# Attention on one core: weights times V as Strassen's seven products in 2x2 blocks, laid between score tiles, with the order of all engines written by hand

## The chip, the cores and the metric

The kernel runs on one core of one Trainium2 chip. The metric is the device time of one launch in microseconds (us), the median over runs; lower is better. The core has a matrix engine (TensorE, PE in the profile; its weight loads are PEld), VectorE (DVE), ScalarE (ACT), GpSimd (POOL) and SyncE (SP); POOL and SP here only issue transfers, apart from a few memsets.

## The reference

```python
scores = np.matmul(q, k.transpose(0, 2, 1)) / np.sqrt(d_k)
attn_weights = special.softmax(scores, axis=-1).astype(np.float32)
return np.matmul(attn_weights, v)
```

q, k and v are float32 of 8 batches x 2048 rows x 512 columns, drawn from a normal distribution. The result is float32 of the same shape.

## The kernel before, in words

Each batch has 16 blocks of 128 rows of K and V (`NKB`), 4 query tiles of 512 rows (`NQT`, `QTW`) and 4 chunks of 128 in the depth of 512 (`ND`). Everything on TensorE is float16, sums are float32.

`prep_dma(b)` asks for a batch's K and Q in two halves each and for V in one piece, through POOL's queue; the transfers turn float32 into float16. V has one more column, set to 1, so that the product with it also gives the row sums of the weights.

`prep_tr(b)` turns K and Q so that depth lies on the partitions: for batch 0 on TensorE (transposes against an identity, lines 83, and a VectorE copy out of PSUM, line 88), for later batches by transposing transfers on SP's queue (line 93), eight per batch, asked for after query tile 0 of the batch before.

`main_batch(b)` goes through the query tiles. For each, 16 score tiles `stp` of 128 x 512 are made by four matmuls each (line 107), and ScalarE writes exp(score / sqrt(512)) into `ptall` as float16 (line 114); there is no subtraction of a maximum. Then for each of four row blocks of 128 queries (`qs`), 32 matmuls add up weights times V over the 16 K blocks in two PSUM banks: line 126 for 257 columns with the column of ones, line 130 for the other 256. VectorE takes the reciprocal of the row sum (line 135), scales 512 columns (line 138) and SP's queue stores the block (line 140).

The pools have 3 score tiles, 2 pairs of output banks, 1 bank for transposes, 2 buffers of `ptall` and 4 of the scaled output. The Tile framework sets the semaphores and orders each engine's instructions by priority; within TensorE all scores of a query tile come ahead of its products with V.

Of the kernel before, what the change touches and what calls it, by code (L numbers as in the profile page):

```python
# [1 line left out]

# [1 line left out]

# [5 lines left out]


@with_exitstack
def kernel(
    ctx: ExitStack,
    tc: tile.TileContext,
    q: bass.AP,
    k: bass.AP,
    v: bass.AP,
    out: bass.AP,  # L20
):
    nc = tc.nc
    P = 128
    B, T, D = q.shape
    F16 = mybir.dt.float16
    F32 = mybir.dt.float32

    NKB = T // P
    ND = D // P
    QTW = 512  # L30
    NQT = T // QTW
    NQS = QTW // P
    NB_ = 256
    NA_ = D + 1 - NB_
    inv_sqrt_d = float(1.0 / np.sqrt(D))
    GP = min(8, NKB)
    NG = NKB // GP

    const = ctx.enter_context(tc.tile_pool(name="const", bufs=1))
    prep_pool = ctx.enter_context(tc.tile_pool(name="prep", bufs=1))  # L40
    persist = ctx.enter_context(tc.tile_pool(name="persist", bufs=2))
    pt_pool = ctx.enter_context(tc.tile_pool(name="ptp", bufs=2))
    oout_pool = ctx.enter_context(tc.tile_pool(name="oout", bufs=4))
    st_psum = ctx.enter_context(tc.tile_pool(name="st_ps", bufs=3, space=bass.MemoryType.PSUM))
    o_psum = ctx.enter_context(tc.tile_pool(name="o_ps", bufs=2, space=bass.MemoryType.PSUM))
    tr_psum = ctx.enter_context(tc.tile_pool(name="tr_ps", bufs=1, space=bass.MemoryType.PSUM))

    ident = const.tile([P, P], F16)

    prepared = {}  # L50
    TG = 4

    def prep_dma(b):
        qh = prep_pool.tile([P, NKB, D], F16, tag="qh")
        kh = prep_pool.tile([P, NKB, D], F16, tag="kh")
        vh = persist.tile([P, NKB, D + 1], F16, tag="vh")
        nc.vector.memset(vh[:, :, D:D + 1], 1.0)  # L57
        qsrc = q[b].rearrange("(n p) d -> p n d", p=P)
        ksrc = k[b].rearrange("(n p) d -> p n d", p=P)
        vsrc = v[b].rearrange("(n p) d -> p n d", p=P)  # L60
        for g in range(NG):
            ts = slice(g * GP, (g + 1) * GP)
            nc.gpsimd.dma_start(out=kh[:, ts, :], in_=ksrc[:, ts, :])  # L63
            nc.gpsimd.dma_start(out=qh[:, ts, :], in_=qsrc[:, ts, :])  # L64
        nc.gpsimd.dma_start(out=vh[:, :, 0:D], in_=vsrc)  # L65
        prepared[b] = [qh, kh, vh, None, None]

    def prep_tr(b):
        st = prepared[b]
        qh, kh = st[0], st[1]  # L70
        qtT = persist.tile([P, NKB, ND, P], F16, tag="qtT")
        ktT = persist.tile([P, NKB, ND, P], F16, tag="ktT")
        st[3] = qtT
        st[4] = ktT
        if b == 0:
            for g in range(NG):
                for src, dst in ((kh, ktT), (qh, qtT)):
                    for j in range(0, GP, 2):
                        tb = g * GP + j
                        trp = tr_psum.tile([P, 2, ND, P], F16, tag="trp")  # L80
                        for jj in range(2):
                            for dc in range(ND):
                                nc.tensor.transpose(  # L83
                                    trp[:, jj, dc, :],
                                    src[:, tb + jj, dc * P:(dc + 1) * P],
                                    ident,
                                )
                        nc.vector.tensor_copy(out=dst[:, tb:tb + 2], in_=trp[:])  # L88
            return
        for g in range(NKB // TG):  # L90
            ns = slice(g * TG, (g + 1) * TG)
            for src, dst in ((kh, ktT), (qh, qtT)):
                nc.sync.dma_start_transpose(  # L93
                    out=dst[:, ns].rearrange("p n c r -> p (n c) r"),
                    in_=src[:, ns, :].rearrange("p n d -> p (n d)"),
                )

    def main_batch(b):
        if b + 1 < B:
            prep_dma(b + 1)  # L100
        _, _, vh, qtT, ktT = prepared[b]
        for qt in range(NQT):
            ptall = pt_pool.tile([P, NKB, QTW], F16, tag="ptall")
            for kb in range(NKB):
                stp = st_psum.tile([P, QTW], F32, tag="stp")
                for dc in range(ND):
                    nc.tensor.matmul(  # L107
                        stp[:],
                        ktT[:, kb, dc, :],
                        qtT[:, qt * NQS:(qt + 1) * NQS, dc, :],  # L110
                        start=(dc == 0),
                        stop=(dc == ND - 1),
                    )
                nc.scalar.activation(  # L114
                    out=ptall[:, kb, :],
                    in_=stp[:],
                    func=mybir.ActivationFunctionType.Exp,
                    scale=inv_sqrt_d,
                )
            for qs in range(NQS):  # L120
                op = o_psum.tile([P, 2 * 512], F32, tag="op")
                opA = op[:, 512:512 + NA_]
                opB = op[:, 0:NB_]
                for kb in range(NKB):
                    lhs = ptall[:, kb, qs * P:(qs + 1) * P]
                    nc.tensor.matmul(  # L126
                        opA, lhs, vh[:, kb, NB_:NB_ + NA_],
                        start=(kb == 0), stop=(kb == NKB - 1),
                    )
                    nc.tensor.matmul(  # L130
                        opB, lhs, vh[:, kb, 0:NB_],
                        start=(kb == 0), stop=(kb == NKB - 1),
                    )
                rinv = oout_pool.tile([P, 1], F32, tag="rinv")
                nc.vector.reciprocal(out=rinv[:], in_=op[:, 512 + NA_ - 1:512 + NA_])  # L135
                osb = oout_pool.tile([P, D], F32, tag="osb")
                src = op.rearrange("p (a c) -> p a c", c=512)[:, :, 0:NB_]
                nc.vector.tensor_scalar_mul(out=osb[:], in0=src, scalar1=rinv[:])  # L138
                gq = qt * NQS + qs
                nc.sync.dma_start(  # L140
                    out=out[b, gq * P:(gq + 1) * P, :], in_=osb[:]
                )
            if qt == 0 and b + 1 < B:
                prep_tr(b + 1)

    prep_dma(0)
    ident_dram = nc.inline_tensor(
        np.eye(P, dtype=np.float16), name="attn_identity"
    )
    nc.sync.dma_start(out=ident[:], in_=ident_dram.ap())  # L150
    prep_tr(0)
    for b in range(B):
        main_batch(b)


# [1 line left out]
_INS = ['q', 'k', 'v']  # L157
_OUTS = [((8, 2048, 512), 'float32')]


# [23 lines left out]
```

## Time and profile before

| what | before |
|---|---|
| time, median of 3 runs | 936.78 us (936.47 to 937.01) |
| time of the profiled execution | 936.28 us |
| its span, first to last instruction | 934.5 us |
| PE busy | 909.8 us, 97% |
| DVE busy | 128.8 us, 14% |
| ACT busy | 306.9 us, 33% |
| transfers | 114.19 MB, mean 122 GB/s |
| mean granted TensorE clock | 0.996 |

The profile page lists busy time per engine, the chain of work that ended last, and groups of equal instructions by line with their count, busy time and mean duration. [...] SPq and POOLq are the queues of SP and POOL. In a table by stretches (windows) the columns are the stretch, its length, each engine's busy time with its number of instructions in the order PE, PEld, DVE, ACT, POOL, then the granted clock, the mean number for the transfers and GB/s.

### The profile page before, as it was taken

What the parts mean: (1) busy time and instruction counts of PE and PEld (TensorE: products, weight loads), DVE (VectorE), ACT (ScalarE), POOL (GpSimd) and SP (SyncE); (2) the same over time, 40 slices, a digit from 0 to 9 for tenths busy, and PEclk for the clock granted to TensorE, in tenths of its full rate; (3) what the DMA queues carried; (4) which work ended last, traced back from release to release, by engine and by line L of the source; (5) the groups of instructions that cost most, each with busy time, mean ns of one, the idle gap of its engine ahead of it and who ended that gap; (6) DMA issues with size and microseconds to landing.
All of it is one profiled execution on the core that took longest, in us unless ns stands there. A gap on an engine that the chain in (4) does not pass through costs nothing.

```text
span 934.5 us, 13963 instructions
## 1 busy us (share of the span) xinstructions
PE 909.8 (97%) x6272; PEld 610.8 (65%) x6272; DVE 128.8 (14%) x280; ACT 306.9 (33%) x513; POOL 37.5 (4%) x44
## 2 busy tenths in 40 slices
PE   3997999999999999999999999999999999999998
PEld 2666666677666677666677666677666677766676
DVE  2211111111011111101111101111110111111111
ACT  0430444222444222344322344322344322344321
POOL 2101000100001000000001000010000000000000
PEclk9998999999999999999999999999999999999999
DMA  9999939980599417991199901998039411000111
GB/s 167 207 193 194 230 84 180 209 160 34 97 184 220 99 47 128 198 205 57 46 169 188 207 35 49 192 213 167 26 82 188 112 46 46 35 23 34 46 46 46
DMA packets 184908, 114.19 MB, mean 122 GB/s; under 512 B 119312, under 2 KB 168464, under 8 KB 184848
## 3 DMA queue, kind: packets, MB, share of 16 engines
q0 software_dynamic: 49792, 50.33, 34.0%
q1 hardware_dynamic: 135056, 62.96, 29.7%
q8 instruction: 49, 0.80, 0.3%
q14 instruction: 11, 0.09, 0.0%
HBM read 100.70 MB, written 33.55 MB: 144 GB/s over the span
## 4 chain that ended last, share of the span: by engine, by line
PE 90%; DMA 5%; SPq 3%; issue 1%; POOL 0%; DVE 0%; POOLq 0%; DVEq 0%
PE stp L107 44%; PE op L126 23%; PE op L130 23%; DMA kh<-in_k_dram 4%; SPq L93 3%; DMA out_dram<-osb 0%; DVE osb L138 0%; POOL kh L63 0%; POOL qh L64 0%; SPq L140 0%; DVE rinv L135 0%; POOLq L63 0%; DVEq L138 0%; POOLq L168 0%; POOLq L64 0%
## 5 line engine op out<-in xcount | busy, mean ns | idle before, releaser
L114 ACT ACTIVATE ptall<-stp 128x512 f16<-128x512 f32 x512 | 305.7, 597 | 609.0 <-PE stp L107 609.0
L126 PE MATMUL op<-vh,ptall 128*128 128x257 f16 x2048 | 455.3, 274 | 5.1 <-DVE osb L138 5.1
L130 PE MATMUL op<-vh,ptall 128*128 128x256 f16 x2048 | 455.2, 273 | 0.0
L107 PE MATMUL stp<-qtT,ktT 128*128 128x512 f16 x2048 | 450.5, 380 | 0.0
L107 PEld LDWEIGHTS <-ktT 128*128 128x128 f16 x2048 | 200.4, 98 | 233.4 <-issue 1.1
L126 PEld LDWEIGHTS <-ptall 128*128 128x128 f16 x2048 | 199.6, 97 | 36.9 <-DVE osb L138 5.7
L130 PEld LDWEIGHTS <-ptall 128*128 128x128 f16 x2048 | 200.2, 98 | 29.4
L135 DVE RECIPROCAL rinv<-op 128x1 f32<-128x1 f32 x128 | 21.5, 168 | 749.4 <-PE op L130 749.4
L138 DVE TENSOR_SCALAR osb<-op,rinv 128x512 f32<-128x512 f32 x128 | 96.1, 751 | 26.5 <-DMA out_dram<-osb 22.4
L65 POOL DMA_DIRECT2D vh<-in_v_dram x8 | 9.2, 1156 | 481.6 <-DVE osb L138 425.9
L63 POOL DMA_DIRECT2D kh<-in_k_dram x16 | 14.2, 887 | 175.2 <-DMA ktT<-kh 100.9
L83 PE MATMUL trp<-ident,kh 128*128 128x128 f16 x64 | 6.6, 266 | 12.8 <-DMA kh<-in_k_dram 10.5
L83 PEld LDWEIGHTS <-kh 128*128 128x128 f16 x64 | 5.6, 123 | 14.8 <-DMA kh<-in_k_dram 10.5
L64 POOL DMA_DIRECT2D qh<-in_q_dram x16 | 14.2, 886 | 14.6 <-DMA qtT<-qh 9.9
L83 PE MATMUL trp<-ident,qh 128*128 128x128 f16 x64 | 6.5, 262 | 2.3 <-DVE qtT L88 1.6
L83 PEld LDWEIGHTS <-qh 128*128 128x128 f16 x64 | 5.6, 120 | 4.7 <-issue 4.2
L88 DVE COPY ktT<-trp 128x1024 f16<-128x1024 f16 x8 | 5.5, 691 | 17.5 <-PE trp L83 17.5
L88 DVE COPY qtT<-trp 128x1024 f16<-128x1024 f16 x8 | 5.5, 691 | 8.0 <-PE trp L83 8.0
L114 ACT ACT_TABLE_LOAD x1 | 1.3, 1283 | 0.7 <-PEq L168 0.7
L57 DVE MEMSET vh<- 128x16 f16 x8 | 0.6, 72 | 0.9 <-PEq L168 0.9
L168 POOL MEMSET const-float32-0.0<- 128x1 f32 x1 | 0.1, 98 | 0.2 <-issue 0.2
L168 POOL MEMSET const-bfloat16-1.0<- 128x1 bf16 x1 | 0.1, 102 | 0.0
(2 smaller groups left out, 0.2 us busy)
## 6 DMA issues: line engine op xcount, KB each, us to landing
out_dram<-osb SPq DMA_DIRECT2D x128, 256.0 KB, 2.6
kh<-in_k_dram POOLq DMA_DIRECT2D x16, 1024.0 KB, 19.0
qh<-in_q_dram POOLq DMA_DIRECT2D x16, 1024.0 KB, 21.0
vh<-in_v_dram POOLq DMA_DIRECT2D x8, 2048.0 KB, 19.9
ktT<-kh SPq DMA_TRANSPOSE x28, 4.9
qtT<-qh SPq DMA_TRANSPOSE x28, 5.7
ident<-attn_identity SPq DMA_DIRECT2D x1, 32.0 KB, 1.7
```

What stands on the lines that cost most here:

```text
L63: nc.gpsimd.dma_start(out=kh[:, ts, :], in_=ksrc[:, ts, :])
L64: nc.gpsimd.dma_start(out=qh[:, ts, :], in_=qsrc[:, ts, :])
L65: nc.gpsimd.dma_start(out=vh[:, :, 0:D], in_=vsrc)
L83: nc.tensor.transpose(trp[:, jj, dc, :], src[:, tb + jj, dc * P:(dc + 1) * P], ident,)
L88: nc.vector.tensor_copy(out=dst[:, tb:tb + 2], in_=trp[:])
L93: nc.sync.dma_start_transpose(out=dst[:, ns].rearrange("p n c r -> p (n c) r"), in_=src[:, ns, :].rearrange("p n d -> p (n d)"),)
L107: nc.tensor.matmul(stp[:], ktT[:, kb, dc, :], qtT[:, qt * NQS:(qt + 1) * NQS, dc, :], start=(dc == 0), stop=(dc == ND - 1),)
L114: nc.scalar.activation(out=ptall[:, kb, :], in_=stp[:], func=mybir.ActivationFunctionType.Exp, scale=inv_sqrt_d,)
L126: nc.tensor.matmul(opA, lhs, vh[:, kb, NB_:NB_ + NA_], start=(kb == 0), stop=(kb == NKB - 1),)
L130: nc.tensor.matmul(opB, lhs, vh[:, kb, 0:NB_], start=(kb == 0), stop=(kb == NKB - 1),)
L135: nc.vector.reciprocal(out=rinv[:], in_=op[:, 512 + NA_ - 1:512 + NA_])
L138: nc.vector.tensor_scalar_mul(out=osb[:], in0=src, scalar1=rinv[:])
```

## The change

Weights times V is done in 2x2 blocks. For a pair of row blocks (128 queries of the first half of the query tile and 128 of the second, so two pairs, a and b, per tile), with even K blocks against odd ones and the first 256 columns of V against the last, Strassen's method in Winograd's form needs seven block products instead of eight. Sums of the weights (`p_sums`) and of V (`v_sums`) are made on VectorE in float16; the products' sums are partly added up in PSUM (bank x takes products 1, 6, 7 and 4, with a reading by VectorE after 1, 6, 7 and 4; z takes 5 and 3) and partly joined in scaled form by VectorE (`after2` to `after7`). Products are numbered, so `a5` is product 5 of pair a; `t1`, `t2`, `t4` are sums of V, `s1`, `s2`, `s4` of the weights, `c1`, `u2`, `p5` scaled parts in SBUF. The column of ones is kept beside V's last half and beside `t1`.

The order of every engine is the program's order (`manual_schedule`). In each query tile there are 16 slots; slot n issues what `prefetch` has for it, score tile n of the *next* query tile, the weight sums if they are due, and one product from `ORDER`; slots 14 and 15 have no product. The scores of tile 0 run ahead of the loop. K and Q are loaded in quarters, transposed by single transfers at chosen slots (batch 0: K and the first quarter of Q on TensorE, the rest of Q by transfers).

The core of the diff (new lines):

```diff
+    def v_sums(b, part):
+        vh, t1, t2, t4 = vs[b]
+        js = slice(part * NJ // 2, (part + 1) * NJ // 2)
+        b11, b12 = vh[:, js, 0, 0:H], vh[:, js, 0, H:D]
+        b21, b22 = vh[:, js, 1, 0:H], vh[:, js, 1, H:D]
+        nc.vector.tensor_sub(t1[:, js, 0:H], b12, b11)
+        nc.vector.tensor_sub(b12, b22, b12)
+        nc.vector.tensor_sub(t2[:, js], b22, t1[:, js, 0:H])
+        nc.vector.tensor_sub(t4[:, js], b21, t2[:, js])
...
+    def p_sums(g, j0, j1):
+        pt, s1, s2, s4 = pts[g]
+        js = slice(j0, j1)
+        a11, a21 = pt[:, js, 0, 0:QH], pt[:, js, 0, QH:QTW]
+        a12, a22 = pt[:, js, 1, 0:QH], pt[:, js, 1, QH:QTW]
+        nc.vector.tensor_add(s1[:, js], a21, a22)
+        nc.vector.tensor_sub(a21, a11, a21)
+        nc.vector.tensor_sub(s2[:, js], s1[:, js], a11)
+        nc.vector.tensor_sub(s4[:, js], a12, s2[:, js])
...
+            lhs, rhs, dst = {
+                1: (lambda j: pt[:, j, 0, c1], lambda j: vh[:, j, 0, 0:H], "x"),
+                2: (lambda j: pt[:, j, 1, c1], lambda j: vh[:, j, 1, 0:H], "y"),
+                3: (lambda j: s4[:, j, c1], lambda j: vh[:, j, 1, H:D + 1], "z"),
+                4: (lambda j: pt[:, j, 1, c2], lambda j: t4[:, j, :], "x"),
+                5: (lambda j: s1[:, j, c1], lambda j: t1[:, j, 0:H + 1], "z"),
+                6: (lambda j: s2[:, j, c1], lambda j: t2[:, j, :], "x"),
+                7: (lambda j: pt[:, j, 0, c2], lambda j: vh[:, j, 0, H:D], "x"),
+            }[n]
...
+            for j in range(NJ):
+                nc.tensor.matmul(
+                    dst[:, 0:width], lhs(j), rhs(j),
+                    start=(first and j == 0), stop=(j == NJ - 1),
+                    skip_group_check=True,
+                )
...
+        def after5(self):
+            self.r2 = small.tile([P, 1], F32, tag="r2")
+            nc.vector.reciprocal(out=self.r2[:], in_=self.z[:, H:H + 1])
+            self.p5 = self.scaled("p5", self.z[:, 0:H], self.r2)
+        def after3(self):
+            self.r1 = small.tile([P, 1], F32, tag="r1")
+            nc.vector.reciprocal(out=self.r1[:], in_=self.z[:, H:H + 1])
+            self.c1 = self.scaled("c1", self.x[:, 0:H], self.r1)
+            self.o1 = opool.tile([P, D], F32, tag="o")
+        def after2(self):
+            self.final(self.o1[:, 0:H], self.y[:, 0:H], self.r1, self.c1)
+        def after6(self):
+            u2 = self.scaled("u2", self.x[:, 0:H], self.r1)
+            self.final(self.o1[:, H:D], self.z[:, 0:H], self.r1, u2)
+            self.store(self.o1, 0)
+        def after7(self):
+            self.o2 = opool.tile([P, D], F32, tag="o")
+            self.final(self.o2[:, H:D], self.x[:, 0:H], self.r2, self.p5)
+        def after4(self):
+            nc.vector.tensor_scalar_mul(
+                out=self.o2[:, 0:H], in0=self.x[:, 0:H], scalar1=self.r2[:]
+            )
+            self.store(self.o2, 1)
+    ORDER = "a1 a5 b5 a3 b1 a2 a6 b3 a7 b2 b6 a4 b7 b4".split()
+    GROUP = 2
...
+        if qt == 0:
+            if slot == 0:
+                load_v(b)
+                load("k", b, 0)
+                load("q", b, 0)
+                load("k", b, 1)
+                load("q", b, 1)
+        if qt == 1:
+            todo = {1: ("k", 0), 5: ("q", 0), 9: ("k", 1), 13: ("q", 1)}
+            if slot in todo:
+                dma_transpose(todo[slot][0], b, todo[slot][1])
+            if slot == 14:
+                load("k", b, 2)
+                load("k", b, 3)
+                load("q", b, 2)
+                load("q", b, 3)
+        if qt == 2:
+            if slot == 2:
+                v_sums(b, 0)
+            if slot == 6:
+                v_sums(b, 1)
+            todo = {6: ("k", 2), 11: ("k", 3), 15: ("q", 2)}
+            if slot in todo:
+                dma_transpose(todo[slot][0], b, todo[slot][1])
+        if qt == 3:
+            if slot == 4:
+                dma_transpose("q", b, 3)
+    load("k", 0, 0)
+    load("q", 0, 0)
+    load("k", 0, 1)
+    load("k", 0, 2)
+    pe_transpose("q", 0, 0)
+    pe_transpose("k", 0, 0)
+    load("k", 0, 3)
+    load("q", 0, 1)
+    load_v(0)
...
+    for kb in range(NKB):
+        qk_tile(0, kb)
+        if kb % CH == 1 and kb // CH + 1 < NCH:
+            pe_transpose("k", 0, kb // CH + 1)
...
+    p_sums(0, NJ - GROUP, NJ)
+    dma_transpose("q", 0, 1)
+    dma_transpose("q", 0, 2)
+    dma_transpose("q", 0, 3)
+    v_sums(0, 0)
+    v_sums(0, 1)
+    for g in range(NG):
+        pair = {"a": Pair(g, 0), "b": Pair(g, 1)}
+        for slot in range(NKB):
+            prefetch(g, slot)
+            if g + 1 < NG:
+                qk_tile(g + 1, slot)
+                if slot % (2 * GROUP) == 0 and slot:
+                    p_sums(g + 1, slot // 2 - GROUP, slot // 2)
+            if slot < len(ORDER):
+                pair[ORDER[slot][0]].product(int(ORDER[slot][1]))
+        if g + 1 < NG:
+            p_sums(g + 1, NJ - GROUP, NJ)
```

PSUM is laid out anew: 3 banks for scores and transposes, 2 for x, 1 for y, 2 for z. The scaled output has 4 buffers of one row block; the staging of loads has 4 quarters; `kT` and `qT` have 6 quarters each.

More of the change, by code (lines that the diff above doesn't have):

```diff
@@ L26 @@
     F32 = mybir.dt.float32
+    EXP = mybir.ActivationFunctionType.Exp
+    MULT = mybir.AluOpType.mult
+    ADD = mybir.AluOpType.add
     NKB = T // P
@@ L42 @@
[L42 to L46, printed above, removed]
-    ident = const.tile([P, P], F16)
[L50 to L88, printed above, removed]
-            return
[L90 to L153, printed above, removed]
+    stage = ctx.enter_context(tc.tile_pool(name="stage", bufs=4))
+    qkt = ctx.enter_context(tc.tile_pool(name="qkt", bufs=6))
+    vpool = ctx.enter_context(tc.tile_pool(name="vpool", bufs=2))
+    ppool = ctx.enter_context(tc.tile_pool(name="ppool", bufs=2))
@@ new lines, with load @@
+    ctx.enter_context(tc.manual_schedule())
+    ident = const.tile([P, P], F16)
+    ident_dram = nc.inline_tensor(np.eye(P, dtype=np.float16), name="attn_identity")
+    nc.sync.dma_start(out=ident[:], in_=ident_dram.ap())
+    qT, kT = {}, {}
+    staged = {}
+    vs = {}
+    pts = {}
+    srcs = {
+        "k": k.rearrange("b (n p) d -> b p n d", p=P),
+        "q": q.rearrange("b (n p) d -> b p n d", p=P),
+        "v": v.rearrange("b (n p) d -> b p n d", p=P),
+    }
+    def load(what, b, c):
+        t = stage.tile([P, CH, D], F16, tag="stage")
+        nc.gpsimd.dma_start(out=t[:], in_=srcs[what][b, :, c * CH:(c + 1) * CH, :])
+        staged[what, b, c] = t
@@ new lines, in dma_transpose, with pe_transpose @@
+    def dma_transpose(what, b, c):
+        src = staged.pop((what, b, c))
+        t = qkt.tile([P, CH, ND, P], F16, tag=what + "T")
+        nc.sync.dma_start_transpose(
+            out=t[:].rearrange("p n c r -> p (n c) r"),
+            in_=src[:].rearrange("p n d -> p (n d)"),
+        )
+        (kT if what == "k" else qT)[b, c] = t
+    def pe_transpose(what, b, c):
+        src = staged.pop((what, b, c))
+        t = qkt.tile([P, CH, ND, P], F16, tag=what + "T")
+        for n in range(0, CH, 2):
+            tr = ps_st.tile([P, 2, ND, P], F16, tag="st")
+            for m in range(2):
+                for dc in range(ND):
+                    nc.tensor.transpose(
+                        tr[:, m, dc, :], src[:, n + m, dc * P:(dc + 1) * P], ident[:]
+                    )
+            nc.vector.tensor_copy(out=t[:, n:n + 2], in_=tr[:])
+        (kT if what == "k" else qT)[b, c] = t
@@ new lines, in load_v @@
+    def load_v(b):
+        vh = vpool.tile([P, NJ, 2, VP], F16, tag="vh")
+        t1 = vpool.tile([P, NJ, TP], F16, tag="t1")
+        t2 = vpool.tile([P, NJ, H], F16, tag="t2")
+        t4 = vpool.tile([P, NJ, H], F16, tag="t4")
+        nc.gpsimd.memset(vh[:, :, 1, D:D + 1], 1.0)
+        nc.gpsimd.memset(t1[:, :, H:H + 1], 1.0)
+        dst = vh[:].rearrange("p j s d -> p (j s) d")
+        for n in range(0, NKB, CH):
+            nc.gpsimd.dma_start(
+                out=dst[:, n:n + CH, 0:D], in_=srcs["v"][b, :, n:n + CH, :]
+            )
+        vs[b] = (vh, t1, t2, t4)
@@ new lines, in p_sums, with __init__, product, scaled @@
+    def p_sums(g, j0, j1):
[7 more added lines that the diff above has]
+        nc.vector.tensor_sub(s4[:, js], a12, s2[:, js])
+    class Pair:
+        def __init__(self, g, i):
+            self.g, self.i = g, i
+        def product(self, n):
+            g, i = self.g, self.i
+            pt, s1, s2, s4 = pts[g]
+            vh, t1, t2, t4 = vs[g // NQT]
+            c1 = slice(i * P, (i + 1) * P)
+            c2 = slice(QH + i * P, QH + (i + 1) * P)
+            if n == 1:
+                self.x = ps_x.tile([P, 512], F32, tag="x")
+            elif n == 2:
+                self.y = ps_y.tile([P, 512], F32, tag="y")
+            elif n == 5:
+                self.z = ps_z.tile([P, 512], F32, tag="z")
+            lhs, rhs, dst = {
[7 more added lines that the diff above has]
+            }[n]
+            dst = getattr(self, dst)
+            width = H + 1 if n in (3, 5) else H
+            first = n in (1, 2, 5)
+            last = n in (2, 3, 4)
+            for j in range(NJ):
+                nc.tensor.matmul(
+                    dst[:, 0:width], lhs(j), rhs(j),
+                    start=(first and j == 0), stop=(j == NJ - 1),
+                    skip_group_check=True,
+                )
+            getattr(self, f"after{n}", lambda: None)()
+        def scaled(self, tag, src, r):
+            t = small.tile([P, H], F32, tag=tag)
+            nc.vector.tensor_scalar_mul(out=t[:], in0=src, scalar1=r[:])
+            return t
+        def final(self, out_, src, r, other):
+            nc.vector.scalar_tensor_tensor(
+                out=out_, in0=src, scalar=r[:], in1=other[:], op0=MULT, op1=ADD
+            )
+        def store(self, o, half):
+            b, qt = divmod(self.g, NQT)
+            n = qt * NQS + half * (NQS // 2) + self.i
+            nc.sync.dma_start(out=out[b, n * P:(n + 1) * P, :], in_=o[:])
+        def after5(self):
[19 more added lines that the diff above has]
+                out=self.o2[:, 0:H], in0=self.x[:, 0:H], scalar1=self.r2[:]
+            )
+            self.store(self.o2, 1)
@@ new lines @@
+    load("k", 0, 0)
[7 more added lines that the diff above has]
+    load_v(0)
+    NG = B * NQT
+    for kb in range(NKB):
+        qk_tile(0, kb)
+        if kb % CH == 1 and kb // CH + 1 < NCH:
+            pe_transpose("k", 0, kb // CH + 1)
+            if kb // CH == 0:
+                load("q", 0, 2)
+            if kb // CH == 1:
+                load("q", 0, 3)
+        if kb % (2 * GROUP) == 0 and kb:
+            p_sums(0, kb // 2 - GROUP, kb // 2)
```

44 lines of the change are left out of this document (36 added, 8 removed).

## Prediction, made before the changed kernel was run

> **What bounds the kernel now.** I read first the page's busy line and its chain of waits, then the costliest groups, then the chain in order of time, then the timeline around one change from scores to weights times V.
>
> ```profile
> span 934.5 us, 13963 instructions
> PE 909.8 (97%) x6272; PEld 610.8 (65%) x6272; DVE 128.8 (14%) x280; ACT 306.9 (33%) x513; POOL 37.5 (4%) x44
> ...
> PE 90%; DMA 5%; SPq 3%; issue 1%; POOL 0%; DVE 0%; POOLq 0%; DVEq 0%
> ...
> L114 ACT ACTIVATE ptall<-stp 128x512 f16<-128x512 f32 x512 | 305.7, 597 | 609.0 <-PE stp L107 609.0
> L126 PE MATMUL op<-vh,ptall 128*128 128x257 f16 x2048 | 455.3, 274 | 5.1 <-DVE osb L138 5.1
> L130 PE MATMUL op<-vh,ptall 128*128 128x256 f16 x2048 | 455.2, 273 | 0.0
> L107 PE MATMUL stp<-qtT,ktT 128*128 128x512 f16 x2048 | 450.5, 380 | 0.0
> ...
> L88 DVE COPY ktT<-trp 128x1024 f16<-128x1024 f16 x8 | 5.5, 691 | 17.5 <-PE trp L83 17.5
> ```
>
> PE is 97% busy and 90% of the chain; every other engine has slack. So matmuls removed come off the end, and a wait put into PE's stream goes on it. The mean durations overlap (274 ns is latency); the rate is read from the chain:
>
> ```profile
> 93.11 13.81 PE stp L107 x64
> ...
> 121.01 13.81 PE stp L107 x64
> ...
> 902.21 13.81 PE stp L107 x64
> ```
>
> One query tile takes 121.01 - 93.11 = 27.90 us; from 121.01 to 902.21 there are 28 of them without a flaw (781.2 / 28 = 27.90). Of it 13.81 is scores (64 matmuls, 0.216 each; one score tile of 4 is 0.863), and 14.09 is 128 matmuls with V, 0.110 each.
>
> ```profile
> 105.90 1.03 PE L107 MATMUL stp<-qtT,ktT 128*128 128x512 f16 x4
> 106.76 0.27 PE L126 MATMUL op<-vh,ptall 128*128 128x257 f16 x1
> ...
> 120.74 0.27 PE L130 MATMUL op<-vh,ptall 128*128 128x256 f16 x1
> 120.85 1.03 PE L107 MATMUL stp<-qtT,ktT 128*128 128x512 f16 x4
> ```
>
> Both hand-overs are seamless: 105.90 + 0.863 = 106.76, and 120.74 + 0.11 = 120.85. PE also begins with V while the last exp still runs (it ends 0.8 after its scores, row below), so waits go by slices, not by whole tiles.
>
> **The change, part by part.** *Matmuls.* Two pairs of seven products of 8 matmuls are 112 instead of 128 per query tile: 112 x 0.110 = 12.32, a gain of 1.77 each, 56 over 32 tiles. Scores stay.
>
> *Hand-overs.* A tile now has 28 instead of 2. The rows above price one with a met wait at 0; I take 0. Upper end: the 0.2 between a result and the engine that waits for it (next).
>
> *VectorE.* New are four f16 sums of 512 elements after every four score tiles, and nine small operations per pair. What one waits and lasts:
>
> ```profile
> 929.84 0.27 PE L130 MATMUL op<-vh,ptall 128*128 128x256 f16 x1
> 930.15 0.17 DVE L135 RECIPROCAL rinv<-op 128x1 f32<-128x1 f32 x1 [2.57 <-PE op L130]
> 930.35 0.75 DVE L138 TENSOR_SCALAR osb<-op,rinv 128x512 f32<-128x512 f32 x1
> 931.13 0.33 SPq L140 DMA_DIRECT2D out_dram<-osb  x1
> ```
>
> A result reaches VectorE 0.20 after the last matmul's slot (929.84 + 0.11 to 930.15), and VectorE goes on 0.04 after its own. Between 0.17 (one element) and 0.75 (512), a 256-wide read of PSUM is 0.46 by the line through them; I use it for the two-input finals too. For an f16 sum no row exists: as a 512-element f32 row it would be 0.75 (one element per cycle), at nothing per element 0.17; nearest in type is the f16 COPY, whose line (0.17 to 0.69 at 1024) gives 0.43 for 512 and 0.69 for 1024. I take those: four sums are 4 x 0.43 + 3 x 0.04 = 1.84. Per query tile VectorE works 4 x 1.84 + 2 x (2 x 0.17 + 7 x 0.46), about 14.5 of 26 us: not the bound, but its queue is in order, and that makes one wait.
>
> The wait is at the end of the order, `a4 b7 b4`. b4 adds to the bank that b7's final must read first, and only one score tile lies between. Counted from the end of a4 (slot 11): VectorE starts a4's scaling at 0.20, ends 0.66; the four sums of slot 12, queued ahead of b7's final, run 0.70 to 2.54; the final 2.58 to 3.04; PE is released 0.05 later, at 3.09. PE wants b4 after score, b7, score: 0.863 + 0.88 + 0.863 = 2.61. So 0.48 of wait in each of 31 tiles, 14.9 us. Queued behind b4 on PE are the last two score tiles, so the next tile starts late with it. Ends: sums at 0.17 give no wait, at 0.75 a wait of 1.76. The other places have a slot to spare: a6 comes two slots after c1's bank is read, a7 and b7 two after u2's. The tightest is a7 in the third tile, where the V sums of the next batch come in two lots of 4 x 0.69 + 0.12 = 2.88 (slots 2 and 6). From the start of slot 6: a2's final ends at 0.66, the second lot runs 0.70 to 3.58, u2 to 4.08, and PE, released at 4.13, wants a7 at 2 x 1.74 + 0.863 = 4.35: no wait, by 0.2.
>
> *ScalarE.* Exp is 597 ns beside 0.863 of score tile: hidden, also in slots 14 and 15.
>
> *Start.*
>
> ```profile
> 10.48 1.03 PE L83 MATMUL trp<-ident,kh 128*128 128x128 f16 x8 [10.48 <-DMA kh<-in_k_dram]
> ...
> 22.07 1.91 PE L107 MATMUL stp<-qtT,ktT 128*128 128x512 f16 x4
> ...
> 26.92 1.03 PE L107 MATMUL stp<-qtT,ktT 128*128 128x512 f16 x4
> 27.87 0.61 PE L83 MATMUL trp<-ident,kh 128*128 128x128 f16 x8
> 28.31 1.03 PE L107 MATMUL stp<-qtT,ktT 128*128 128x512 f16 x4
> ```
>
> The first K load (1 MB) landed at 10.48; now K and Q of half that size land together by about 10.2. 32 transposes at half speed (1.03 for 8, here without the copy's stall) and the copies: scores begin at 13.75 instead of 22.07. Then 16 score tiles (13.81), 48 transposes at 0.44 per 8 (27.87 to 28.31): 2.6, and 1.0 for tiles still at half clock (the tile at 22.07 took 1.91): the loop begins at 31.2.
>
> ```profile
> 10.00:12.00 2.00, 1.03 (x8) 0.88 (x9) 0.45 (x1) 0.00 (x0) 0.00 (x0) 1.00 1.24 204
> ```
>
> The other K chunks (0.52 MB each, 2.55 us at 204 GB/s) land ahead of their use; V, behind them and Q, lands at about 30.
>
> ```profile
> 27.99 0.60 ACT L114 ACTIVATE ptall<-stp 128x512 f16<-128x512 f32 x1 [0.81 <-PE stp L107]
> ```
>
> This exp ends 0.8 after its score tile (26.92 + 0.863 = 27.78, to 27.99 + 0.60). Counted from the loop's begin: the last sums run to 2.64, the first lot of V sums to 5.56, and the first sum of the second lot, done at 6.29, releases the fifth matmul of a5, which PE wanted at 0.863 + 0.88 + 0.863 + 0.44 = 3.05: 3.3 of wait, once.
>
> *SP and POOL queues.* The same bytes move: loads in quarters, transposes at slots 1 to 15, between stores instead of eight in a row.
>
> ```profile
> ktT<-kh SPq DMA_TRANSPOSE x28, 4.9
> ```
>
> ```profile
> PE op L126 <- DVE osb L138: 5.1, 2, 4.5
> ```
>
> Before, stores stuck behind those eight kept output buffers busy and PE idle for 4.5 us once. Now each transpose (4.9 to landing) has four slots (7 us); a store is late by one of them at most, and its four output buffers give it a whole tile. K, Q and V of a batch (4 MB with V, 20 us at 204) are asked for a tile (26 us) ahead of the first transpose, and that a tile ahead of its first score. The late quarters K2, K3, Q2, Q3 wait on POOL for staging buffers that transposes free, with nothing behind them until the next batch; K2 waits on SP for score slot 3 of its own tile, three slots before. Price 0; without that cover, 4.5 us and half a clock for 6 us after it (its rows stand below), some 7.5 per batch.
>
> *Sum.* 31.2 + 3.3 + 31 x (13.81 + 12.32 + 0.48) + 12.32 (last tile, no scores) + 0.75 (b4 there: b7 + 0.20, final 0.46, 0.05) + 4.1 (scaling 0.66, then 931.13 to 934.5) = 876.6 of span. The profiled run took 936.28 against a span of 934.5, and lies 0.5 under the median: 878.9, so 879.
>
> **The rivals.** *No wait at b4* (864): if the sums last 0.31 or less, the final is done before PE comes; 879 - 14.9. [...]
>
> *VectorE at one element per cycle* (965, slower): sums at 0.75 make the b4 wait 1.76 (+40), the V sums 5.5 a lot, which come behind sums already late by 3.7 and keep u2 from a7 until 10.4 into slot 6, 6.0 past its time, in seven batches (+42), and the start 4.5 longer. It decides from about 0.64 per sum. For it: the f32 row. Against: the f16 COPY moved 1024 in 0.69.
>
> *Hand-overs cost* (905): 0.03 at each of 868 would be 26; from 0.067 on the gain is gone. Against: both seams above.
>
> *SP late* (some 930 at 7.5 in seven batches, 910 in four): for it, the 4.5 us wait; against, the spread.
>
> ```profile
> 82.00:84.00 2.00, 1.72 (x9) 1.22 (x10) 0.29 (x2) 0.00 (x0) 0.00 (x0) 0.50 0.96 183
> ...
> 88.00:90.00 2.00, 1.35 (x13) 0.93 (x11) 0.82 (x2) 0.00 (x0) 0.88 (x1) 0.99 1.10 192
> ```
>
> *The clock falls* (966): after the 4.5 us idle PE ran at 0.50 until about 88, some 5.6 us; the same behind every b4 wait would cost 2.8 x 31 = 87. [...] Against: in the row 88.00:90.00 PE idled 0.65 and held 0.99.
>
> **How the numbers follow.** Chances: forecast 0.45, no wait at b4 0.22, hand-overs 0.15, SP late 0.08, one element per cycle 0.07, clock 0.03. The forecast's own range is 872 to 888. Outside 860 to 908 I leave 0.10 for the two slow cases, 0.06 for costlier hand-overs and SP, 0.04 below. 0.2% (1.9 us) is about what a measurement of this kernel tells from no change; slower: 0.07 + 0.03 + 0.01 of the hand-overs; same 0.02; faster 0.87.
>
> **What would show it.** Right: 3584 matmuls with V at 0.110; query tiles 26.6 apart; PE idle ahead of the product with `t4`, released by VectorE's final, 0.5 each 31 times; sums at 0.43; first scores before 15 us; one wait of about 3 near 33 us. Wrong: tiles 26.1 apart (sums are cheaper), idle at every product start (hand-overs), PE waiting for `kT` or `qT`, a clock under 1.00 in the loop, or sums over 0.6.

## The result and the profile after

The changed kernel takes 871.88 us (median of 4 runs, 870.88 to 872.42) against 936.87 for the kernel before; the ratio is 0.9306 (95% interval 0.929 to 0.9322), 65 us less. The profiled execution took 872.25 with a span of 870.3, so all sums below go to 870.3.

The page of the changed kernel, the same parts as before: span, busy time by engine, the chain by engine, and the groups that carry the argument. Line 142 is now the scores, line 193 every product, lines 155 to 158 the weight sums, line 202 a scaling and line 206 a final (the operation that scales a product and adds a scaled part to it).

```profile
span 870.3 us, 13872 instructions
PE 846.7 (97%) x5712; PEld 557.3 (64%) x5712; DVE 475.1 (55%) x1162; ACT 307.0 (35%) x513; POOL 72.7 (8%) x116
...
PE 95%; DMA 4%; DVE 0%; issue 0%; POOL 0%; ACT 0%; POOLq 0%
...
L142 PE MATMUL st<-t 128*128 128x512 f16 x2048 | 514.9, 380 | 9.4 <-DMA t<-t 9.1
...
L202 DVE TENSOR_SCALAR t<-x,r 128x256 f32<-128x256 f32 x128 | 61.9, 484 | 72.0 <-PE x L193 69.7
L155 DVE TENSOR_TENSOR s<-pt 128x512 f16<-128x512 f16 x128 | 53.5, 418 | 64.7 <-ACT pt L146 64.7
...
L206 DVE SCALAR_TENSOR_TENSOR o<-y,r,t 128x256 f32<-128x256 f32 x64 | 30.9, 484 | 57.8 <-PE y L193 57.8
```

TensorE is still the bound, with 560 fewer instructions (512 of the products, 48 transposes), and VectorE went from 14% to 55% without taking its place. An f16 sum of 512 takes 0.42 and a 256-wide read of PSUM 0.484. The scores show 514.9 us where they showed 450.5, though they issue as fast as before (12 in 2.59 in the chain below, 0.216 each): each tile's last matmul now overlaps with a product's first (the score tile at 428.69 lasts 1.03, and the product behind it starts at 429.55), and the sum of the lines counts the overlap twice. Rates must again be read from the chain. Its pieces of 12 score matmuls are slots 14 and 15 of one tile and slot 0 of the next; from the piece of tile 0 to that of tile 29:

```profile
65.91 2.59 PE st L142 x12
...
825.15 2.59 PE st L142 x12
```

29 tiles in 759.24 us: 26.18 each, where the tile before took 27.90. Slot 14 starts 24.45 into a tile (26.18 less two score tiles), so the first piece says that the loop ran as if it had begun without a flaw at 65.91 - 24.45 = 41.46 by the chain. The chain puts a piece that follows another without a wait 0.16 later than the timeline does (121.01 against 120.85 in the prediction's lines), so by the timeline it is 41.30. What lies ahead of that is the start, and the chain shows what held it:

```profile
13.26 8.98 DMA t<-in_q_dram
22.24 0.02 issue
22.25 16.93 DMA t<-t
39.19 0.05 issue
39.23 1.89 PE st L142 x4
```

Q1, the second quarter of batch 0's Q, was asked for at 13.26 and landed at 22.24. Its transposing transfer was issued at 22.25 and landed 16.93 us later. TensorE had finished the scores of tile 0 at 30.16 and waited 9.07 for it. The windows of the wait and of the loop behind it (stretch, length, busy time of PE, PEld, DVE, ACT, POOL, then the granted clock):

```profile
30.16:39.23 9.07, 0.00 (x1) 0.00 (x0) 6.87 (x12) 0.60 (x1) 0.00 (x0) 0.67 0.95 148
39.23:67.64 28.41, 28.41 (x177) 18.05 (x178) 11.81 (x30) 8.96 (x15) 6.14 (x11) 0.93 1.15 178
67.64:853.03 785.39, 785.39 (x5282) 516.37 (x5281) 436.47 (x1076) 286.56 (x480) 57.99 (x89) 1.00 0.69 131
```

The granted clock fell during the wait, from 1.00 at 30 to 32 us to 0.50 at 34 to 36, and stayed low for some 4 us behind it: 0.50 at 40 to 42, 0.64 at 42 to 44, 1.00 at 44 to 46 (41.30 - 39.23 = 2.07 lost). From 67.64 to 853.03 PE is busy without a gap that the view counts, at a granted clock of 1.00.

### The profile page after: what moved, and what is told of

Same layout as the page of the kernel before. It is cut to its first block, busy times and chain, and to the rows that moved or that the text cites. A ratio compares the mean times of both kernels' runs of the same rounds, so it can differ in the third digit from the quotient of the medians.

```text
span 870.3 us, 13872 instructions
## 1 busy us (share of the span) xinstructions
PE 846.7 (97%) x5712; PEld 557.3 (64%) x5712; DVE 475.1 (55%) x1162; ACT 307.0 (35%) x513; POOL 72.7 (8%) x116
## 4 chain that ended last, share of the span: by engine, by line
PE 95%; DMA 4%; DVE 0%; issue 0%; POOL 0%; ACT 0%; POOLq 0%
PE st L142 49%; PE x L193 26%; PE z L193 13%; PE y L193 6%; DMA t<-t 2%; DMA t<-in_q_dram 2%; PE tr L100 0%; POOL t L81 0%; ACT pt L146 0%; DVE o L206 0%; DVE t L202 0%; DVE o L239 0%; DVE s L155 0%; DVE pt L156 0%; DVE s L158 0%
## 5 line engine op out<-in xcount | busy, mean ns | idle before, releaser
L142 PE MATMUL st<-t 128*128 128x512 f16 x2048 | 514.9, 380 | 9.4 <-DMA t<-t 9.1
L146 ACT ACTIVATE pt<-st 128x512 f16<-128x512 f32 x512 | 305.7, 597 | 546.0 <-PE st L142 546.0
L142 PEld LDWEIGHTS <-t 128*128 128x128 f16 x2048 | 200.4, 98 | 159.1 <-DMA t<-t 9.6
L193 PEld LDWEIGHTS <-pt 128*128 128x128 f16 x2048 | 200.5, 98 | 81.5 <-issue 8.6
L193 PEld LDWEIGHTS <-s 128*128 128x128 f16 x1536 | 150.3, 98 | 58.2 <-issue 0.5
L193 PE MATMUL x<-vh,pt 128*128 128x256 f16 x1024 | 133.6, 274 | 0.0
L193 PE MATMUL z<-vh,s 128*128 128x257 f16 x512 | 66.7, 273 | 0.4 <-DVE t L202 0.4
L193 PE MATMUL z<-t,s 128*128 128x257 f16 x512 | 66.6, 273 | 0.0
L193 PE MATMUL y<-vh,pt 128*128 128x256 f16 x512 | 66.4, 273 | 0.0
L193 PE MATMUL x<-t,s 128*128 128x256 f16 x512 | 66.4, 273 | 0.0
```

Of the source, the lines that this page charges most:

```text
L142: nc.tensor.matmul(st[:], kT[b, c][:, n, dc, :], qT[b, qt][:, :, dc, :], start=(dc == 0), stop=(dc == ND - 1),)
L146: nc.scalar.activation(out=pt[:, kb // 2, kb % 2, :], in_=st[:], func=EXP, scale=inv_sqrt_d)
L193: nc.tensor.matmul(dst[:, 0:width], lhs(j), rhs(j), start=(first and j == 0), stop=(j == NJ - 1), skip_group_check=True,)
```

## The experiments

Three questions: what of the 65 us is the seven products and what the new layout; why the wait at b4, forecast at 0.48 a tile, is hardly there; and what held the start.

**Eight products in the new layout.** `a1` to `b4` replaced by sixteen half-products without any sums. A class of ordinary products stands in for the pairs; its `product(slot)` does the row block `slot // 4`, one half of V and one half of the K blocks, 8 matmuls. The call:

```diff
-            if slot < len(ORDER):
-                pair[ORDER[slot][0]].product(int(ORDER[slot][1]))
...
+            plain.product(slot)
```

> The new layout (score tiles of the next tile laid between the products, order by hand, start, loads) with the eight ordinary products and no sums on VectorE: 16 half-products of 8 matmuls per query tile, one in each slot. Theory A (the seven products are the gain, the layout adds only the earlier start): a query tile takes 13.81 + 128 x 0.1093 = 27.8 instead of 26.18, the wait for Q1's transposing transfer stays, so 870.3 + 31 x (27.8 - 26.18) + 1 = about 921 of span, 923 of time, 14 under the kernel before. Rival B (the layout itself is worth much of the 65 us): under 905. Rival C (28 hand-overs cost something that the sums hid): over 935.

Measured: 923.07 (922.55 to 924.09), ratio 0.9857 (0.984 to 0.9873). Two rows of its timeline, fifteen slots apart:

```profile
401.37 1.04 PE L252 MATMUL acc<-vh,pt 128*128 128x256 f16 x8
...
427.47 1.04 PE L252 MATMUL acc<-vh,pt 128*128 128x256 f16 x8
```

26.10 / 15 = 1.74 a slot, 27.84 a tile. So of the 65 us the layout and the new start are 14 and the seven products 51. The tiles account for the 51: 31 x (27.84 - 26.18) = 51.5, and 0.5 more in the last tile, less 1.0 because this kernel's loop begins earlier (the product of slot 1 at 42.92, in the changed kernel at 43.89). Of the 14 only 32 x (27.90 - 27.84) = 2 lies in the tiles; the rest is the start, the wait of 4.5 us that the kernel before had near its 80th us with the low clock behind it (0.50 from 82 to 88 us), and 0.5 at the end. Theory A holds; B and C fall.

**The sums twice.** Four more sums per group, into scratch, ahead of the real ones:

```diff
...
+        nc.vector.tensor_add(d1[:, 0:n], a21, a22)
+        nc.vector.tensor_sub(d2[:, 0:n], a11, a21)
+        nc.vector.tensor_sub(d3[:, 0:n], d1[:, 0:n], a11)
+        nc.vector.tensor_sub(d4[:, 0:n], a12, d3[:, 0:n])
         nc.vector.tensor_add(s1[:, js], a21, a22)
```

> All weight sums of each group made twice, first into scratch that nobody reads: four more f16 operations ahead of b7's final in VectorE's queue. Theory A (b4 waits for b7's final, which waits in order behind the sums): the wait at b4 grows from 0.12 by four more sums of 1.58 together to 1.7 per query tile, 31 x 1.58 = 49 more; with the V sums in seven batches and the start a few more: 922 to 930 of time. Rival B (VectorE's place in the queue does not hold TensorE): 872 to 876, no wait ahead of the product with t4.

Measured: 919.27, one run. Its TensorE around b7 and b4:

```profile
421.74 1.04 PE L203 MATMUL x<-vh,pt 128*128 128x256 f16 x8
422.61 1.03 PE L143 MATMUL st<-t 128*128 128x512 f16 x4
425.06 0.38 PE L203 MATMUL x<-t,pt 128*128 128x256 f16 x2 [1.42 <-DVE o L216]
```

The wait stands where theory A puts it, ahead of the product with `t4`, released by VectorE's final, in each tile. b4 begins at 425.06 where 422.61 + 0.863 = 423.47 was its time: 1.59 late, against 1.70 expected, since the four extra sums put b7's final back by 1.47 and not 1.58. The time is 3 under the expected range; the V sums brought little: in the third tile of the first batch a7 starts 0.19 late (110.28 instead of 109.23 + 0.863), the place that the prediction called the tightest. B falls: VectorE's queue does hold TensorE there.

**The sums of slot 12 behind b7's final.**

```diff
-                if slot % (2 * GROUP) == 0 and slot:
+                if slot in (4, 8):
                     p_sums(g + 1, slot // 2 - GROUP, slot // 2)
             if slot < len(ORDER):
                 pair[ORDER[slot][0]].product(int(ORDER[slot][1]))
+            if g + 1 < NG and slot == 12:
+                p_sums(g + 1, slot // 2 - GROUP, slot // 2)
```

> The weight sums of slot 12 are issued behind b7's final instead of ahead of it. Theory A: b4's wait of 0.12 per query tile is gone, 31 x 0.12 = 3.7 us: 868 of time, tiles 26.06 apart. Rival B (the wait is between b7's final and b4 by itself, not by the queue): within 0.5 of 871.9.

Measured: 867.69 (867.37 to 868.36), ratio 0.9265 (0.9253 to 0.9278). Its chain, 27 tiles apart:

```profile
116.89 2.59 PE st L142 x12
...
820.69 2.59 PE st L142 x12
```

703.80 / 27 = 26.07 a tile, 0.11 less, 3.5 over 31 tiles: that was the whole wait at b4, and it is gone. The rest of the 4.2 is in the start, which no edit touched here: the scores of tile 1 begin at 38.42 instead of 39.23. Theory A.

**Scores first, then products.** The product taken out of each slot and all fourteen put behind the slots:

```diff
-            if slot < len(ORDER):
-                pair[ORDER[slot][0]].product(int(ORDER[slot][1]))
...
+        for slot in range(len(ORDER)):
+            pair[ORDER[slot][0]].product(int(ORDER[slot][1]))
```

> In each query tile all 16 score tiles of the next one first, then the 14 products back to back: 2 hand-overs instead of 28, nothing between products. Theory A (a hand-over costs nothing and the score tiles hide VectorE's reads): every query tile gets the waits that the last one shows now (0.54 at a3, 0.73 at b4): 13.81 + 12.25 + 1.2 = 27.2 instead of 26.18, 903 to 906 of time. Rival B (hand-overs cost 0.03 or more each): 26 x 0.03 = 0.8 of that comes back, under 882.

Measured: 907.52, one run. Its waits of TensorE and its chain:

```profile
PE x L193 <- DVE o L206: 18.5, 32, 0.6
PE z L193 <- DVE t L202: 11.3, 31, 0.4
```

```profile
123.53 13.83 PE st L142 x64
...
861.42 13.83 PE st L142 x64
```

737.89 / 27 = 27.33 a tile, 1.15 more than laid between (0.13 more than expected, so the time is 1.5 over the range). Its two waits account for all of it: read from the starts in the timeline they are 0.53 ahead of a3 and 0.75 ahead of b4, and 13.81 + 12.25 + 1.28 = 27.34. With 2 hand-overs a tile instead of 28 nothing comes back: a hand-over costs nothing that can be seen, and a score tile between products is what hides VectorE's reads. B falls.

**V's loads behind Q1's transposing transfer.** A memset on POOL, which waits for that transfer, stands ahead of them:

```diff
     load("q", 0, 1)
+    q1_staged = staged["q", 0, 1]
+    dma_transpose("q", 0, 1)
+    nc.gpsimd.memset(q1_staged[:, 0, 0:8], 0.0)
     load_v(0)
...
-    dma_transpose("q", 0, 1)
```

> Batch 0's V loads are asked for only when Q1 is transposed (a memset of Q1's staged tile on POOL waits for the transposing transfer). Theory A (that transfer took 17 us because it shared the transfer engines with V's loads): it lands 5 to 7 us after its issue and its issue comes sooner (Q1 at about 17 instead of 22.25), so the score tile 1 starts at 30 without a wait and the wait moves to V, which comes at about 34 to 36. Rival B (the first transposing transfer is slow by itself): 15 us or more from issue to landing again, and V as late as 42 or more, time over 874.

Measured: 873.75, one run. Its chain:

```profile
22.48 4.37 DMA t<-t
...
29.66 11.44 DMA vh<-in_v_dram
41.10 0.04 issue
41.14 0.59 PE x L193 x2
```

The same transfer, with nothing of V beside it, took 4.37 us instead of 16.93. So it is not slow by itself: the 16.93 came beside V's loads and Q2's behind them on POOL's queue, which the edit moves together, and theory B on the cause falls. Two of A's times were wrong: Q1 itself landed at about 22.5 as before (K1 to K3 are ahead of it, not V), and V came only at 41.1, so the wait moved to a1 and the time did not improve. Either order needs K, Q0, Q1 and V on the chip before a5, and one of them is last.

**Q1 on TensorE.** 16 transposes behind score tile 13 in place of the transposing transfer:

```diff
+        if kb == 13:
+            pe_transpose("q", 0, 1)
...
-    dma_transpose("q", 0, 1)
```

> Q1 of batch 0 transposed on TensorE after score tile 13, in place of the transposing transfer. Theory A (the loop starts 9.07 late because of that transfer, and the idle halves the clock for 4 us more, 2.2 lost): scores of tile 1 start at about 31, and the next to be late is V's sums on VectorE, whose second lot releases a5's fifth matmul at about 36.5 where TensorE wants it at 34: 2 to 3 of wait, too short to drop the clock. 41.46 becomes about 34: 863 of span, 864 to 866 of time. Rival B (V's landing holds the loop start anyway): V lands at 35 and a1 waits, gain under 4.

Measured: 865.06 (864.85 to 867.17), ratio 0.9241 (0.9229 to 0.9254), 6.8 under the changed kernel. The start now waits for the V sums, as theory A has it; its waits of TensorE, and two windows of the profiled execution:

```profile
PE z L193 <- DVE t L125: 2.3, 2, 2.0
```

```profile
36.00:38.00 2.00, 0.70 (x5) 0.53 (x5) 1.97 (x4) 0.00 (x0) 0.00 (x0) 0.93 1.25 207
38.00:40.00 2.00, 2.00 (x7) 0.84 (x6) 1.83 (x4) 0.29 (x1) 0.00 (x0) 0.50 1.23 204
```

That 2 to 3 us of wait are too short to drop the clock was A's estimate: the clock held in three executions (mean granted clock 1.0, 864.9 to 865.2), and fell in the profiled one (0.997, 867.17).

**All three.** Q1 on TensorE, the sums of slot 12 behind b7's final, and `v_sums(0, 0)` behind Q1's transposes instead of behind the last weight sums.

> Q1 of batch 0 on TensorE, the sums of slot 12 behind b7's final, and the first lot of batch 0's V sums ahead of the last weight sums. Theory A (the start's waits and b4's are separate and add): 7.5 + 3.7 + up to 2 of a5's wait: 858 to 861 of time. Rival B (what one edit frees, V's landing takes back): 864 to 868.

Measured: 859.94 (859.51 to 860.94), ratio 0.9185 (0.9173 to 0.9198). Its chain, with tiles 703.80 / 27 = 26.07 apart, and the one wait left between the scores of tile 0 and the loop:

```profile
109.08 2.59 PE st L142 x12
...
812.88 2.59 PE st L142 x12
```

```profile
PE z L193 <- DVE t L125: 0.8, 1, 0.8
```

The gains add: 6.8 from Q1, 3.5 from the tiles and 1.5 from the shorter wait at a5 (2.3 to 0.8) make 11.8, and 11.9 were measured. The third edit was not run alone. This is the fastest version run, 12 under the changed kernel.

## Why the prediction was right, and where it was off

The 871.88 lies 7.1 under the forecast of 879, inside the range of 860 to 908 and 0.1 under the 872 to 888 of the likeliest case, for the reason given: matmuls taken off TensorE come off the end. But two terms of the sum were wrong, in opposite directions, and that they cancel by half is luck.

| term | forecast | measured |
|---|---|---|
| products of a tile | 12.32 | 26.07 - 13.81 = 12.26 |
| hand-overs | 0 | none seen |
| wait at b4, each tile | 0.48 | 0.11 |
| 31 tiles | 824.9 | 811.6 |
| scores begin | 13.75 | 13.00 |
| scores of tile 0 end | 31.2 | 30.16 |
| wait at the start | 3.3 | 9.07, and 2.07 by the clock |
| loop begins in effect | 34.5 | 41.30 |
| last tile and tail | 17.2 | 17.4 |

Tiles 13.3 less, start 6.8 more, end 0.2 more: 876.6 became 870.3. The half clock in the forecast's 1.0 for slow score tiles is shown by no run: the tile at 22.07 of the kernel before took its 1.91 with the granted clock at 1.00, and in the changed kernel no score tile was slow at the start, the first two going from 13.00 to 14.74, 0.87 each. Two of the prediction's own signs of being wrong came: tiles nearer 26.1 than 26.6 apart, though each sum lasts what was forecast, and TensorE waiting once for `qT`.

*The wait at b4* was mis-sized, not misplaced. The sum of a chain of six VectorE operations had a gap of 0.04 behind each, taken from a reciprocal and the scaling that needs it. The changed kernel's VectorE between a4 and b4:

```profile
428.89 0.48 DVE L239 TENSOR_SCALAR o<-x,r 128x256 f32<-128x256 f32 x1 [0.73 <-PE x L193]
429.29 0.41 DVE L155 TENSOR_TENSOR s<-pt 128x512 f16<-128x512 f16 x1
429.74 0.42 DVE L156 TENSOR_TENSOR pt<-pt 128x512 f16<-128x512 f16 x1
430.08 0.42 DVE L157 TENSOR_TENSOR s<-s,pt 128x512 f16<-128x512 f16 x1
430.53 0.42 DVE L158 TENSOR_TENSOR s<-pt,s 128x512 f16<-128x512 f16 x1
430.87 0.48 DVE L206 SCALAR_TENSOR_TENSOR o<-x,r,t 128x256 f32<-128x256 f32 x1
```

```profile
430.42 1.03 PE L142 MATMUL st<-t 128*128 128x512 f16 x4
431.41 0.38 PE L193 MATMUL x<-t,pt 128*128 128x256 f16 x2
```

Each duration is within 0.03 of the forecast. But an operation that neither needs what the one in front of it writes nor overwrites what that one reads starts 0.08 before that one's end (429.29 against 428.89 + 0.48; 430.08 against 429.74 + 0.42). Only the second sum, which overwrites what the first read, and the fourth, which needs what the third wrote, wait 0.03 to 0.04. Three of the five gaps were -0.08 instead of 0.04, which is 0.36 of the 0.37 by which the chain came out shorter: a4 ends at 428.69, the final ends at 431.35, and b4 starts at 431.41, 2.72 behind a4 instead of the forecast 3.09. Without a wait it would have started at 430.42 + 0.863 = 431.28. The doubled sums and the moved ones show that this queue is the cause. The doubled sums also set the two kinds of gap side by side, with the same first two sums once into scratch and once as they are:

```profile
421.48 0.41 DVE L161 TENSOR_TENSOR d<-pt 128x512 f16<-128x512 f16 x1
421.81 0.42 DVE L162 TENSOR_TENSOR d<-pt 128x512 f16<-128x512 f16 x1
...
422.94 0.42 DVE L165 TENSOR_TENSOR s<-pt 128x512 f16<-128x512 f16 x1
423.39 0.42 DVE L166 TENSOR_TENSOR pt<-pt 128x512 f16<-128x512 f16 x1
```

Into scratch the second sum starts 0.33 behind the first; where it writes over what the first reads, 0.45.

The rival *no wait at b4* was therefore nearly true in its place, but not for its condition, sums of 0.31 or less: the sums take 0.42.

*The start* failed in the step on the SP and POOL queues: "Price 0". It looked at the later batches, where the spread holds (no wait for a transposed quarter after 39.23), and gave batch 0 no line, though there Q1's transposing transfer is issued into V's loads, with the loop waiting for it. The row of 4.9 us to landing is a median; beside V's loads one such transfer took 16.93. The kernel before had shown the spread in its view of line 93, its transposing transfers:

```profile
DMA to landing us min/median/max: 4.4/5.1/19.5
```

The rival *SP late* named this kind of wait and put it into the wrong batch. The forecast 3.3 of wait at a5 was real in kind, hidden behind the longer one: with Q1 on TensorE, TensorE waited 2.3 there.

*Hand-overs*, *one element per cycle* (a name for sums of 0.75, as long as the f32 row of 512; no run shows a cycle) and *the clock falls* did not come: sums are at 0.42, and the loop's window holds a granted clock of 1.00 with 0.11 of wait a tile. With the doubled sums TensorE waits some 1.6 a tile, and the mean granted clock of that run is 0.997, not under the changed kernel's 0.994.

*Not forecast*: 0.53 of wait at a3 in the last tile, where the last weight sums meet products without score tiles between them; products 0.1 shorter and a tail 0.2 shorter make up for part of it.

## What to carry to other kernels

When work moves to an engine with slack, price its in-order queue at the one place where the bound engine waits for it, with gaps from rows of the same dependence: operations that need each other and operations that do not are priced apart (gaps of 0.03 to 0.04 and -0.08 here). Look for that place by asking which two uses of one buffer lie closest together, and move what is queued between them; here that is 3.5 us for one moved call. At the start of a kernel, do not price a transfer by its median time to landing (4.9 us here, where the one that held the loop took 16.93): look at the largest too, ask what else is on the transfer engines when it is issued, and whether the bound engine can do the same job itself in its shadow (6.8 us here).

## What the runs showed of the hardware that was not expected

- In the chains shown, VectorE starts an operation 0.08 us before the end of the one in front where they are independent, and 0.03 to 0.04 after it where it needs that one's result or overwrites its input.
- A transposing transfer of one quarter (0.5 MB) took 4.37 us without V's loads and 16.93 beside loads that keep the transfer engines at 195 to 199 GB/s (26 to 36 us of the changed kernel).
- Idle of 0.26 and 2.04 us, with 0.6 us of work between, came with a fall of the granted clock to 0.50 for some 3.5 us (0.93 at 36 to 38 us, 0.50 at 38 to 40, 0.72 at 40 to 42) in one execution out of four of the kernel with Q1 on TensorE, which took 2 us longer; in the other three the mean clock was 1.0. It was 0.50 behind the 4.5 us of the kernel before (82 to 88 us) and behind the 9.07 here; around the 0.8 at the start of the fastest version it was 1.00 (30 to 40 us), and with 1.42 in each tile under the doubled sums its mean over the run was 0.997.
